# Exchanging 32x32 blocks through device memory in place of transposes on the tensor engine

## The chip, the cores and the metric

The kernel runs on one core of a Trainium2 chip. The metric is the device time of one execution in microseconds (us). A core has a tensor engine (PE, with PEld for its weight loads), a vector engine (DVE), a scalar engine (ACT), GpSimd (POOL) and a sync engine (SP), each with an instruction stream of its own that it works off in order, and 16 DMA engines that move data between device memory and the on-chip buffers.

## The reference

256 tokens of width 2048 go through one transformer block and then two further layers. All weights are float32 and each is used once. In outline:

```
x = x + merged(heads(norm(x) @ w_in)) @ w_out      # 16 MLA heads and 16 forget-gate (fox) heads
x = x + peer(norm(x))                              # product keys over 16384 experts
for layer in 0, 1:
    aq ak av ag bq bk bv bg cu cglu cg = split(x @ w_in2)
    ya = diff_attention(aq, ak, av) * silu(ag)     # 4 heads of 128
    yb = dilated_attention(bq, bk, bv) * silu(bg)  # 8 heads of 128
    yc = conv_module(cu, cglu) * silu(cg)
    x = layer_norm(alpha * x + concat(ya, yb, yc) @ w_out2)
```

In the first block the outputs of the two attentions are multiplied by a sigmoid of a gate before `w_out`; in the layers the outputs of the three branches by a silu. The attention needs queries and keys with the head's dimension on the partitions, and each product with a weight needs its left operand with the contracted dimension on the partitions. Projections come out with the tokens on the partitions, so a block of 256 tokens x 512 columns has to be transposed before it serves as either.

## The kernel before

The weights stream through in 561 jobs, each a tile `raw` of 128 x 2048 floats (1 MB), loaded by SP four tiles ahead. A tile is worked in 4 pieces of 512 columns, 2244 pieces in all. For each piece ACT casts the weights to a short float (`hi`, L208), DVE takes the rest (`lo` = raw - hi, L209), and PE makes three products for each of the two blocks of 128 tokens: hi with the activations' upper part (L260), lo with it (L261), hi with their lower part (L263). Eight buffers for hi and for lo let ACT and DVE run up to 7 pieces ahead of PE.

Everything else (attention, norms, transposes, gates) is side work, written as Python generators. A planner, `Tasks`, takes one step (a tick) after each piece and writes out the next part of at most one task of each of its 4 lanes, so the order on every engine is fixed in advance: `yield n` lets n ticks pass, `apart` is the number of ticks after a task before those that need it may start, and a job that needs a result `flush`es what is left of its task at once. A tick is thus a place in the program, one piece of weights wide.

The change touches these pieces of side work. `transposed` (L223 to L231) transposes four 128x128 blocks at a time on PE into a PSUM tile `side` (L230, 8 instructions for 256 tokens x 512 columns), and hands each of two such tiles on. `to_heads` (L504 to L512) copies these tiles out on ACT, as queries or keys of four heads; `fox_norm`, the MLA tasks `post_q` and `post_k` and the layers' `heads_post` (L1109) call it. `merged_task` (L700) copies gated outputs out as an upper and a lower part, on ACT (L212) and DVE (L213). `split_scaled` and `split` are such pairs of instructions, with and without a factor. `exchange` works in the manner of code that already stands in the part on the experts: two 32x32-block transposes on DVE (L946), a write to device memory (`ad`, L948) and four reads (L957) that bring the blocks back in their transposed places. The softmax of a head (`softmax_block`, L531 to L535) runs on DVE and ACT, with an exponential on ACT between two DVE rows; L1149, L1188, L1152 to L1156 and L1194 belong to the layers' heads, L1224 and L1227 are the taps of the convolution, and L1253 to L1258 the activation after its norm, with ACT and DVE in turn.

Of the kernel before, what the change touches and what calls it, by code (L numbers as in the profile page):

```python
# [110 lines left out]
def hybrid_block_kernel(ctx: ExitStack, tc: tile.TileContext, a: dict, out: bass.AP):  # L111
# [46 lines left out]
    cst = kept([256], name="cst")  # L158
    A.dma_start(out=cst, in_=a["cst"][:, 0:256])
# [11 lines left out]
    ident, maskf = cst[:, 0:128], cst[:, 128:256]  # L171
# [4 lines left out]
    for c0 in (0, 256):  # L176
        V.tensor_copy(out=causal[:, c0:c0 + 128], in_=maskf)
# [291 lines left out]
    def forget_bias(g):  # L469
# [4 lines left out]
        mask = maskf[:, None, :].to_broadcast([P, 4, P])  # L474
# [29 lines left out]
    def to_heads(raw, gain):  # L504

        dst = s4([4, T])
        for pv, c in transposed(lambda c, tb: raw[:, tb, c * P:(c + 1) * P], 4):
            if gain is None:
                A.copy(out=dst[:, c:c + 2, :], in_=pv)
            else:  # L510
                A.activation(out=dst[:, c:c + 2, :], in_=pv, func=AF.Copy, scale=gain)
        return dst  # L512

    def fox_norm(key, raw, gain, post):
        def work():
# [5 lines left out]
            S[key] = to_heads(raw, gain)  # L521
# [34 lines left out]
    def attention(parts, b0, b1, v, y, h):  # L556
# [10 lines left out]
        for tb in range(TB):  # L567
            V.tensor_scalar(out=y[:, tb, h * P:(h + 1) * P], in0=o[:, tb * P:(tb + 1) * P], scalar1=rs[:, tb:tb + 1],
                            scalar2=None, op0=OP.mult)
# [59 lines left out]
    def mla_group(g):  # L629
# [13 lines left out]
        def post_q(ps):  # L643
# [3 lines left out]
            def work():  # L647
# [11 lines left out]
                S["mq", g] = (to_heads(raw, vcol("mq")), rope_T(qr, False))  # L659
# [3 lines left out]
        def post_k(ps):  # L663
# [3 lines left out]
            def work():  # L667
# [11 lines left out]
                S["mk", g] = (to_heads(raw, vcol("mk")), rope_T(kr, True))  # L679
# [20 lines left out]
    def merged_task(key, m, scale):  # L700

        h, l = s4([4, T], F32R), s4([4, T], F32R)
        S[key] = (h, l)

        def work():
            for pv, c in transposed(lambda c, tb: m[:, tb, c * P:(c + 1) * P], 4):
                split_scaled(h[:, c:c + 2, :], l[:, c:c + 2, :], pv, scale)
            yield END
        S[key + ("t",)] = tasks.add(work(), apart=7, lane=1)

    def gate_jobs(kind, g):
# [9 lines left out]
        def post(ps):  # L721
# [7 lines left out]
            merged_task(("m" + kind, g), z, 0.5)  # L729
# [91 lines left out]
    def peer_q_jobs():  # L821
# [5 lines left out]
        for b in range(4):  # L827
            def post(ps, b=b):
# [3 lines left out]
                def work():  # L832
                    qT = to_heads(raw, None)
# [271 lines left out]
    def layer(ly):  # L1105
# [504 lines left out]
```

## Time and profile before

| | |
|---|---|
| time, median of 3 runs | 3291.41 us (3290.26 to 3292.29) |
| the profiled execution: time, span | 3291.13 us, 3289.3 us |
| PE busy | 3258.4 us, 99% of the span |
| PEld busy | 2706.2 us, 82% |
| DVE busy | 2360.8 us, 72% |
| ACT busy | 1748.4 us, 53% |
| POOL busy | 644.8 us, 20% |
| mean granted clock of PE | 0.997 |

The span runs from the first to the last instruction of the core; the profiled execution took 1.83 us more than its span. Busy shares are means over the whole span: an engine at 72% may be full in one stretch and idle in another. Matmuls overlap, so the time that one costs is read from the distance between starts.

### The profile page before, as it was taken

The page shows a single profiled execution, that of the slowest core. Times are in us where ns is not written, and L with a number is a line of the kernel's source. Part 1 is how long each engine was busy: PE and PEld are TensorE (multiplying, and loading weights), DVE is VectorE, ACT ScalarE, POOL GpSimd, SP SyncE. Part 2 cuts the span into 40 slices and gives each one's busy share as a digit, 9 for nine tenths or more (in the row PEclk, how much of TensorE's full clock was granted, in tenths as well). Part 3 has the DMA queues.
Part 4 walks back from the last instruction along what each step waited for, and adds up shares of the span by engine and source line. Part 5 has one row for each costly group of instructions (what it writes and reads, how often), then busy time and mean ns, then how long its engine had stood idle before and what let it go on. Part 6 is the DMA issues. An engine that isn't in the chain of part 4 may idle for free.

```text
span 3289.3 us, 42994 instructions
## 1 busy us (share of the span) xinstructions
PE 3258.4 (99%) x15019; PEld 2706.2 (82%) x15020; DVE 2360.8 (72%) x4733; ACT 1748.4 (53%) x3061; POOL 644.8 (20%) x590
## 2 busy tenths in 40 slices
PE   9999999999999999999999999999999999999997
PEld 7878888888888888888888888888888888788886
DVE  6677676776678888555676766767668777778767
ACT  6655555554655555555554444444555554455553
POOL 0000000000007787876232222220000000000001
PEclk9999999999999999999999999999999999999999
DMA  6544555678557788777788777776564456444454
GB/s 246 174 151 160 182 186 173 210 263 281 174 181 213 216 225 222 212 217 218 258 261 250 238 253 243 231 241 209 203 219 167 154 181 207 171 167 165 172 192 141
DMA packets 159897, 676.54 MB, mean 206 GB/s; under 512 B 52000, under 2 KB 68784, under 8 KB 88128
## 3 DMA queue, kind: packets, MB, share of 16 engines
q1 hardware_dynamic: 102416, 613.06, 55.0%
q0 software_dynamic: 56832, 60.45, 8.7%
q8 instruction: 117, 1.92, 0.2%
q14 instruction: 100, 0.82, 0.1%
q10 hardware_dynamic: 432, 0.29, 0.0%
HBM read 635.58 MB, written 38.15 MB: 205 GB/s over the span
## 4 chain that ended last, share of the span: by engine, by line
PE 98%; DVE 1%; ACT 0%; issue 0%; DMA 0%; DVEq 0%; SPq 0%; ACTq 0%
PE acc L263 31%; PE acc L260 31%; PE acc L261 31%; PE side L230 2%; PE side L576 2%; PE side L542 1%; PE side L552 0%; PE side L553 0%; PE side L551 0%; DVE lo L209 0%; PE side L839 0%; DVE X L1328 0%; DMA X<-in_x_dram 0%; DVE lst L1314 0%; DVE X L295 0%
## 5 line engine op out<-in xcount | busy, mean ns | idle before, releaser
L209 DVE TENSOR_TENSOR lo<-raw,hi 128x512 fp32r<-128x512 f32 x2244 | 1502.5, 688 | 713.0 <-ACT hi L208 699.1
L208 ACT CAST hi<-raw 128x512 fp32r<-128x512 f32 x2244 | 1369.5, 622 | 1166.5 <-DVE lo L209 596.3
L260 PE MATMUL acc<-hi,xh 128*128 128x512 f32 x2816 | 1119.2, 397 | 2.0 <-ACT xh L1362 0.9
L261 PE MATMUL acc<-lo,xh 128*128 128x512 f32 x2816 | 1097.3, 390 | 4.9 <-DVE lo L209 4.9
L263 PE MATMUL acc<-hi,xl 128*128 128x512 f32 x2816 | 1097.9, 390 | 2.9 <-DVE xl L209 2.8
L260 PE MATMUL acc<-hi,s 128*128 128x512 f32 x1664 | 654.3, 393 | 0.0
L261 PE MATMUL acc<-lo,s 128*128 128x512 f32 x1664 | 647.6, 389 | 0.0
L263 PE MATMUL acc<-hi,s 128*128 128x512 f32 x1664 | 646.0, 389 | 0.0
L263 PEld LDWEIGHTS acc<-hi,xl 128*128 128x128 f32 x2816 | 529.0, 188 | 116.1 <-DVE xl L209 4.1
L261 PEld LDWEIGHTS acc<-lo,xh 128*128 128x128 f32 x2816 | 529.7, 188 | 111.3 <-DVE lo L209 6.3
L260 PEld LDWEIGHTS acc<-hi,xh 128*128 128x128 f32 x2816 | 529.5, 188 | 108.3 <-ACT xh L1362 1.6
L914 POOL DMA_INDIRECT gd<-pick x256 | 430.3, 1681 | 93.7 <-issue 74.6
L263 PEld LDWEIGHTS acc<-hi,s 128*128 128x128 f32 x1664 | 312.4, 188 | 65.3
L261 PEld LDWEIGHTS acc<-lo,s 128*128 128x128 f32 x1664 | 312.6, 188 | 63.4
L260 PEld LDWEIGHTS acc<-hi,s 128*128 128x128 f32 x1664 | 312.5, 188 | 63.1
L1339 POOL TENSOR_TENSOR X<-X,s 128x512 f32<-128x512 f32 x6 | 9.0, 1525 | 875.9 <-ACT X L1338 875.9
L957 POOL DMA_DIRECT2D s<-ad x128 | 77.1, 622 | 407.2 <-PE acc L263 189.2
L535 ACT ACTIVATE s<-s,sm 128x128 f32<-128x128 f32 (+1 forms) x128 | 57.2, 448 | 123.3 <-DVE sm L533 123.3
L1227 DVE SCALAR_TENSOR_TENSOR s<-s,vec,s 128x256 f32<-128x256 f32 x240 | 115.5, 481 | 4.5
L948 POOL DMA_DIRECT2D ad<-s x32 | 28.7, 898 | 365.4 <-DVE s L946 364.4
L960 POOL DMA_DIRECT2D s<-gd x128 | 90.5, 713 | 19.1 <-DMA s<-gd 7.7
L984 DVE TENSOR_TENSOR X<-X,acc 128x512 f32<-128x512 f32 x128 | 81.9, 681 | 0.0
(257 smaller groups left out, 1675.1 us busy)
## 6 DMA issues: line engine op xcount, KB each, us to landing
raw<-in_ut_dram SPq DMA_DIRECT2D x128, 1024.0 KB
raw<-in_pv_dram SPq DMA_DIRECT2D x128, 1024.0 KB
raw<-in_w_dram SPq DMA_DIRECT2D x120, 1024.0 KB
raw<-in_win_dram SPq DMA_DIRECT2D x87, 1024.0 KB
raw<-in_wout_dram SPq DMA_DIRECT2D x32, 1024.0 KB
raw<-in_wo_dram SPq DMA_DIRECT2D x32, 1024.0 KB
gd<-s SPq DMA_DIRECT2D x16, 1024.0 KB
raw<-in_wpq_dram SPq DMA_DIRECT2D x16, 1024.0 KB
```

Source lines behind the costliest of these rows:

```text
L208: A.copy(out=hi, in_=src)
L209: V.tensor_tensor(out=lo, in0=src, in1=hi.bitcast(F32), op=OP.subtract)
L230: PE.transpose(pv[:, i, tb * P:(tb + 1) * P], src_of(c + i, tb), ident)
L260: PE.matmul(ps[tb], lhsT=lh[:, kc, t], rhs=wh, start=start, stop=False)
L261: PE.matmul(ps[tb], lhsT=lh[:, kc, t], rhs=wl, start=False, stop=False)
L263: PE.matmul(ps[tb], lhsT=ll[:, kc, t], rhs=wh, start=False, stop=stop)
L576: PE.matmul(sc[:, o0:o0 + k1], lhsT=q[:, q0:q0 + P], rhs=k[:, 0:k1], start=i == 0, stop=i == len(parts) - 1)
L914: G.indirect_dma_start(out=gd.rearrange("p i (n o) -> (p i n) o", o=1), out_offset=bass.IndirectOffsetOnAxis(ap=pick[:, 1, h, k:k + 1].bit ...
L957: G.dma_start(out=aT[32 * q:32 * q + 32], in_=S["ad", g][:, :, q].rearrange("(i r) t x -> r t i x", i=4))
L960: G.dma_start(out=gg[:, q], in_=gd[:, :, g * 4 * 32:(g + 1) * 4 * 32])
L984: V.tensor_tensor(out=X[:, tb, c], in0=X[:, tb, c], in1=ps[tb], op=OP.add)
L1227: V.scalar_tensor_tensor(out=cv[:, c], in0=pad[:, k:k + T], scalar=tapw(k), in1=cv[:, c], op0=OP.mult, op1=OP.add)
```

## The change

A new function `exchange` stands for the PE transposes in `to_heads` and `merged_task`. It transposes the source in blocks of 32x32 on DVE, two instructions of 128x512; writes the result to device memory from POOL's queue (512 KB); reads it back in four transfers of 128 KB into 32 partitions each, into the same buffer; and lets 12 ticks pass. ACT, and for gated outputs DVE, then copy from that buffer in SBUF instead of from PSUM, in one instruction of 128x1024 where there were two of 128x512. 44 blocks go this way: 8 of fox queries and keys, 8 of MLA queries and keys, 12 of the layers' heads, 8 gate merges and 8 merges in the layers. The gated outputs are therefore copied without a factor (but for `oa`), and the factor 0.5 goes into instructions that scale anyway. `merged_task` keeps its successors 2 ticks away instead of 7. At the start a 64 KB load brings the identity alone, and the masks come by two more DMAs instead of two DVE copies. The transposes of the activations, the latents, the rotated parts, the convolution and the experts' queries stay on PE.

```diff
+    def exchange(src):
+        gt = s4([TB, 4, 4, 32])
+        mem = dram.tile([P, TB, 4, P], F32, name=nm("xm"))
+        for tb in range(TB):
+            V.transpose(out=gt[:, tb].rearrange("p q b c -> p b q c"), in_=src[:, tb])
+        G.dma_start(out=mem, in_=gt.rearrange("p t q b c -> p t q (b c)"))
+        back = gt.rearrange("p t i b c -> p t i (b c)")
+        for q in range(4):
+            G.dma_start(out=back[32 * q:32 * q + 32], in_=mem[:, :, q].rearrange("(i r) t x -> r t i x", i=4))
+        yield 12
+        return back.rearrange("p t i (b c) -> p (t i) b c", b=4)
...
-    def to_heads(raw, gain):
-        dst = s4([4, T])
-        for pv, c in transposed(lambda c, tb: raw[:, tb, c * P:(c + 1) * P], 4):
-            if gain is None:
-                A.copy(out=dst[:, c:c + 2, :], in_=pv)
-            else:
-                A.activation(out=dst[:, c:c + 2, :], in_=pv, func=AF.Copy, scale=gain)
-        return dst
+    def to_heads(raw, *gains):
+        back = yield from exchange(raw)
+        dsts = [s4([4, T]) for _ in gains]
+        for dst, gain in zip(dsts, gains):
+            copy_scaled(by_32(dst), back, gain)
+        return dsts if len(dsts) > 1 else dsts[0]
...
-    def merged_task(key, m, scale):
-        h, l = s4([4, T], F32R), s4([4, T], F32R)
-        S[key] = (h, l)
+    def merged_task(key, m, scale=None):
         def work():
-            for pv, c in transposed(lambda c, tb: m[:, tb, c * P:(c + 1) * P], 4):
-                split_scaled(h[:, c:c + 2, :], l[:, c:c + 2, :], pv, scale)
+            back = yield from exchange(m)
+            h, l = s4([4, T], F32R), s4([4, T], F32R)
+            S[key] = (h, l)
+            if scale is None:
+                split(by_32(h), by_32(l), back)
+            else:
+                for b in range(4):
+                    split_scaled(by_32(h)[:, :, b], by_32(l)[:, :, b], back[:, :, b], scale)
             yield END
-        S[key + ("t",)] = tasks.add(work(), apart=7, lane=1)
+        S[key + ("t",)] = tasks.add(work(), apart=2, lane=1)
...
-        def heads_post(name, gain):
+        def heads_post(name, *gains):
...
-                    if name != "ak":
-                        L[name] = to_heads(raw, gain)
-                    else:
-                        L[name] = [s4([4, T]), s4([4, T])]
-                        for pv, c in transposed(lambda c, tb: raw[:, tb, c * P:(c + 1) * P], 4):
-                            for i in range(2):
-                                copy_scaled(L[name][i][:, c:c + 2, :], pv, halves[:, i:i + 1])
+                    L[name] = yield from to_heads(raw, *gains)
                     yield END
                 L[name + "_t"] = tasks.add(work(), apart=11)
```

Since the planner waits in ticks, other side work moves against the weights' pieces. Lines of the changed kernel lie 18 or 19 further down in the layers (L531 is L549, L1152 is L1171, L1227 is L1246) and one up near the start (L209 is L208).

On POOL, in the first block after the write of the forget-gate sums (`fd`), the old order goes on to loads of these sums and of gate biases:

```order
L466 DMA fd<-s_223_999 16x256
L472 DMA s_287_1271<-fd 128x1024
L472 DMA s_587_2441<-fd 128x1024
L719 DMA s_692_2828<-in_bgate_dram 128x512
L719 DMA s_758_3109<-in_bgate_dram 128x512
L472 DMA s_939_3857<-fd 128x1024
```

and in the changed order, at the same place (`xm` is an exchange's tile in device memory, `s` the buffer in SBUF):

```order
L465 DMA fd<-s_223_999 16x256
L513 DMA xm_1156<-s_259_1155 128x1024
L516 DMA s_259_1155<-xm_1156 32x8x128 x4
L471 DMA s_286_1267<-fd 128x1024
L513 DMA xm_1364<-s_308_1363 128x1024
L516 DMA s_308_1363<-xm_1364 32x8x128 x4
```

Exchanges now stand between them; the four reads of an exchange follow its write directly, so on POOL they wait for it.

On DVE, in layer 0, the first place is where the differential heads' two softmaxes are put together (L1152 to L1156; `raw`, `lo` and `hi` are the weights, the other names buffers). Before:

```order
L209 TENSOR_TENSOR lo_23357<-raw_23107,hi_23356 128x512
L209 TENSOR_TENSOR lo_23367<-raw_23107,hi_23366 128x512
L1152 TENSOR_SCALAR sm_23320<-sm_23320,lam_21940 128x2
L1154 TENSOR_SCALAR s_5409_23321<-s_5409_23321,sm_23320 128x128
L1156 SCALAR_TENSOR_TENSOR s_5392_23269<-s_5392_23269,sm_23268,s_5409_23321 128x128
L1154 TENSOR_SCALAR s_5409_23321<-s_5409_23321,sm_23320 128x256
L1156 SCALAR_TENSOR_TENSOR s_5392_23269<-s_5392_23269,sm_23268,s_5409_23321 128x256
L1227 SCALAR_TENSOR_TENSOR s_5182_22342<-s_5154_22236,vec_90,s_5182_22342 128x256 x2
L209 TENSOR_TENSOR lo_23387<-raw_23107,hi_23386 128x512
```

and in the changed order:

```order
L208 TENSOR_TENSOR lo_23436<-raw_23193,hi_23435 128x512
L512 STREAM_TRANSPOSE s_5452_23445<-s_5395_23239 128x4x4x32 x2
L208 TENSOR_TENSOR lo_23455<-raw_23193,hi_23454 128x512
L1171 TENSOR_SCALAR sm_23399<-sm_23399,lam_21884 128x2
L1173 TENSOR_SCALAR s_5439_23400<-s_5439_23400,sm_23399 128x128
L1175 SCALAR_TENSOR_TENSOR s_5422_23348<-s_5422_23348,sm_23347,s_5439_23400 128x128
L1173 TENSOR_SCALAR s_5439_23400<-s_5439_23400,sm_23399 128x256
L1175 SCALAR_TENSOR_TENSOR s_5422_23348<-s_5422_23348,sm_23347,s_5439_23400 128x256
L1246 SCALAR_TENSOR_TENSOR s_5182_22286<-s_5155_22181,vec_90,s_5182_22286 128x256 x2
L208 TENSOR_TENSOR lo_23472<-raw_23193,hi_23471 128x512
```

The two transposes of a key or query block (L512) stand between two weight pieces ahead of L1171. One convolution row, L1224, which came 7 rows further on before, no longer follows.

The second place on DVE is in layer 0 between the statistics of the convolution's norm and its use, before:

```order
L209 TENSOR_TENSOR lo_24624<-raw_24375,hi_24623 128x512
L1194 TENSOR_SCALAR s_5638_24322<-side_24633,sm_24387 128x128 x2
L209 TENSOR_TENSOR lo_24640<-raw_24375,hi_24639 128x512
L1194 TENSOR_SCALAR s_5638_24322<-side_24649,sm_24411 128x128 x2
L209 TENSOR_TENSOR lo_24656<-raw_24375,hi_24655 128x512
L1194 TENSOR_SCALAR s_5638_24322<-side_24665,sm_24437 128x128 x2
L209 TENSOR_TENSOR lo_24672<-raw_24375,hi_24671 128x512
L1194 TENSOR_SCALAR s_5638_24322<-side_24683,sm_24461 128x128 x2
```

and in the changed order, from the transposes of the gated output `oa` on:

```order
L512 STREAM_TRANSPOSE s_5689_24468<-s_5677_24434 128x4x4x32 x2
L1258 BN_STATS sm_24478<-side_24479 128x6
L1259 BN_AGGR sm_24478<-sm_24478 128x2
L1258 BN_STATS sm_24478<-side_24487 128x6
L1259 BN_AGGR sm_24478<-sm_24478 128x2
L208 TENSOR_TENSOR lo_24496<-raw_24304,hi_24495 128x512
L549 ISA s_5700_24510,sm_24511<-side_24505,s_5174_22252 128x128
L549 ISA sm_24511 128x1
L549 ISA s_5700_24510,sm_24511<-side_24505,s_5174_22252 128x256
L549 ISA sm_24511 128x1
L551 TENSOR_SCALAR sm_24512<-sm_24511 128x2
L1207 RECIPROCAL sm_24509<-sm_24508 128x2
```

In place of the last scalings of heads that were done (L1194) stand the softmaxes of the last four heads (L549 to L1207), one between each pair of weight pieces; two rows L213 that followed before are gone, and three copies L562 (L544 before) come in ahead of L1272 (L1253 before). The number of weight pieces in the stretch is the same, and five of them in a row now come ahead of it where there were two between the last copy L544 and it.

## Rows read from the trace of the kernel before

**Rows 1.** The page: busy us and share by engine; the chain that ended last.

```profile
PE 3258.4 (99%) x15019; PEld 2706.2 (82%) x15020; DVE 2360.8 (72%) x4733; ACT 1748.4 (53%) x3061; POOL 644.8 (20%) x590
...
PE 98%; DVE 1%; ACT 0%; issue 0%; DMA 0%; DVEq 0%; SPq 0%; ACTq 0%
```

**Rows 2.** Waits of PE over the span: line, releaser, us in total, times, longest.

```profile
PE acc L261 <- DVE lo L209: 4.9, 4, 2.9
```

**Rows 3.** PE by line and form: instructions, busy us, mean ns; then the chain.

```profile
L230 PE MATMUL side<-cst,s 128*128 128x128 f32 x464 | 59.5, 272 | 0.0
...
478.28 1.31 PE side L230 x12
```

**Rows 4.** Timeline of PE around one group of transposes: start us, us, line.

```profile
340.65 1.04 PE L230 MATMUL side<-cst,s 128*128 128x128 f32 x8
341.44 0.48 PE L260 MATMUL acc<-hi,xh 128*128 128x512 f32 x1
341.76 0.39 PE L261 MATMUL acc<-lo,xh 128*128 128x512 f32 x1
341.99 0.39 PE L263 MATMUL acc<-hi,xl 128*128 128x512 f32 x1
```

**Rows 5.** DVE by line and form: count, busy us, mean ns, idle before it.

```profile
L209 DVE TENSOR_TENSOR lo<-raw,hi 128x512 fp32r<-128x512 f32 x2240 | 1500.8, 688 | 713.0 <-ACT hi L208 699.1 <-issue 7.6 <-ACT s L940 1.9
...
L946 DVE STREAM_TRANSPOSE s<-s 128x512 f32<-128x512 f32 x64 | 45.2, 707 | 6.9 <-ACT s L940 2.6 <-issue 2.0 <-DMA gd<-pick 1.3
...
L544 DVE COPY s<-side 128x384 f32<-128x384 f32 x56 | 30.9, 553 | 1.0 <-PE side L542 1.0
```

**Rows 6.** One group of ACT, in the same columns.

```profile
L208 ACT CAST s<-s 128x1024 fp32r<-128x1024 f32 x32 | 33.6, 1050 | 60.6 <-DVE s L969 56.8 <-DMA s<-ad 1.9 <-DMA s<-gd 1.9
```

**Rows 7.** Timeline rows of POOL: a write and reads of device memory.

```profile
2393.96 0.71 POOL L1064 DMA_DIRECT2D skew<-s  x1 [5.40 <-ACT s L1063]
...
2398.60 0.75 POOL L1070 DMA_DIRECT2D s<-skew  x1 [2.43 <-DMA skew<-s]
...
1685.16 2.42 POOL L957 DMA_DIRECT2D s<-ad  x4 [10.35 <-PE acc L263]
...
1693.27 0.59 POOL L957 DMA_DIRECT2D s<-ad  x1 [1.46 <-DMA s<-ad]
```

**Rows 8.** Timeline of DVE, then PE, after layer 0's differential softmaxes.

```profile
2513.78 0.28 DVE L531 CUSTOM_DVE_ANT_0 s<-side,s 128x128 f32<-128x128 f32 x1
...
2515.67 0.17 DVE L1149 RECIPROCAL sm<-sm 128x2 f32<-128x2 f32 x1 [1.06 <-ACT s L535]
2516.18 1.29 DVE L209 TENSOR_TENSOR lo<-raw,hi 128x512 fp32r<-128x512 f32 x2 [0.35 <-ACT hi L208]
...
2522.79 0.41 DVE L1224 TENSOR_SCALAR s<-s,vec 128x256 f32<-128x256 f32 x1
...
2524.15 1.89 DVE L209 TENSOR_TENSOR lo<-raw,hi 128x512 fp32r<-128x512 f32 x3
...
2525.26 0.39 PE L261 MATMUL acc<-lo,xh 128*128 128x512 f32 x1
```

**Rows 9.** The same, where four softmaxes of heads b0 end.

```profile
2561.10 1.29 DVE L209 TENSOR_TENSOR lo<-raw,hi 128x512 fp32r<-128x512 f32 x2
...
2563.39 0.39 PE L261 MATMUL acc<-lo,xh 128*128 128x512 f32 x1
```

**Rows 10.** Timeline of DVE, then PE, at layer 0's convolution norm.

```profile
2645.24 0.60 DVE L1194 TENSOR_SCALAR s<-side,sm 128x128 f32<-128x128 f32 x2
...
2653.00 1.41 DVE L213 SCALAR_TENSOR_TENSOR s<-side,hg,s 128x512 fp32r<-128x512 f32 x2
...
2656.12 0.99 DVE L1253 TENSOR_SCALAR s<-side,vec 128x256 f32<-128x256 f32 x2
...
2663.51 4.30 DVE L209 TENSOR_TENSOR lo<-raw,hi 128x512 fp32r<-128x512 f32 x7
...
2664.64 0.39 PE L261 MATMUL acc<-lo,s 128*128 128x512 f32 x1
```

More of the change, by code (lines that the diff above doesn't have):

```diff
@@ L157, in hybrid_block_kernel @@
     X = res.tile([P, TB, D], F32, name="X")
-    cst = kept([256], name="cst")
-    A.dma_start(out=cst, in_=a["cst"][:, 0:256])
+    ident = kept([128], name="ident")
+    A.dma_start(out=ident, in_=a["cst"][:, 0:128])
     warm = s2([512], BF16)
@@ L176, in hybrid_block_kernel @@
     for c0 in (0, 256):
-        V.tensor_copy(out=causal[:, c0:c0 + 128], in_=maskf)
+        A.dma_start(out=causal[:, c0:c0 + 128], in_=a["cst"][:, 128:256])
     halves = kept([2], name="halves")
@@ L473, in forget_bias @@
         yield 8
-        mask = maskf[:, None, :].to_broadcast([P, 4, P])
+        mask = causal[:, None, 0:P].to_broadcast([P, 4, P])
         V.tensor_tensor(out=f0, in0=f[:, :, 0:P], in1=mask, op=OP.add)
@@ L520, in work @@
             yield
-            S[key] = to_heads(raw, gain)
+            S[key] = yield from to_heads(raw, gain)
             yield END
@@ L568, in attention @@
             V.tensor_scalar(out=y[:, tb, h * P:(h + 1) * P], in0=o[:, tb * P:(tb + 1) * P], scalar1=rs[:, tb:tb + 1],
-                            scalar2=None, op0=OP.mult)
+                            scalar2=0.5, op0=OP.mult, op1=OP.mult)
         yield END
@@ L658, in work @@
                 yield 9
-                S["mq", g] = (to_heads(raw, vcol("mq")), rope_T(qr, False))
+                qr = rope_T(qr, False)
+                S["mq", g] = ((yield from to_heads(raw, vcol("mq"))), qr)
                 yield END
@@ L678, in work @@
                 yield 9
-                S["mk", g] = (to_heads(raw, vcol("mk")), rope_T(kr, True))
+                kr = rope_T(kr, True)
+                S["mk", g] = ((yield from to_heads(raw, vcol("mk"))), kr)
                 yield END
@@ L728, in post @@
             V.scalar_tensor_tensor(out=z, in0=z, scalar=1.0, in1=y, op0=OP.add, op1=OP.mult)
-            merged_task(("m" + kind, g), z, 0.5)
+            merged_task(("m" + kind, g), z)
         block_jobs([a["win"][b, k] for k in range(4)], post, pre=pre)
@@ L832, in work @@
                 def work():
-                    qT = to_heads(raw, None)
+                    qT = s4([4, T])
+                    for pv, c in transposed(lambda c, tb: raw[:, tb, c * P:(c + 1) * P], 4):
+                        A.copy(out=qT[:, c:c + 2, :], in_=pv)
                     yield
@@ L1264, in pw_post @@
         def pw_post(ps):
-            L["yc"] = raw_of(ps)
+            L["yc"] = raw_of(ps, lambda tb: 0.5)
             L["c_t"] = []
@@ L1299, in layer @@
         outs(0, "oa", first=ALPHA)
-        blk(11, lambda ps: silu_gate(ps, lambda: L["yb", 1], "ob1", 0.5, "b1"))
+        blk(11, lambda ps: silu_gate(ps, lambda: L["yb", 1], "ob1", None, "b1"))
         outs(1, "ob0")
```

15 lines of the change are left out of this document (8 added, 7 removed).

## The prediction

> **What bounds the kernel now.** I read the page's busy shares and the chain first: PE is busy for 99% of the span and carries 98% of the chain [rows 1]. Work taken off PE therefore shortens the time, as long as PE isn't made to wait instead. So the second view is PE's waits: its only mentionable wait on DVE's lower parts is 4.9 us in 4 pieces [rows 2]. The third is DVE, which the change loads. Of its idle time in front of L209, 713.0 us, 699.1 end with ACT's cast [rows 5]: over most of the span DVE has done everything that there is, the eight buffers are full, and it runs at PE's pace. There an added microsecond on DVE costs nothing. But a mean over the span doesn't tell this of a single stretch, so the fourth view sets a weight piece's end on DVE beside its use on PE, at the places where side work is densest. After the differential heads' softmaxes in layer 0, DVE's first of three L209 ends 0.69 us after 2524.15, at 2524.84, and PE uses it at 2525.26 [rows 8]: 0.42 us to spare. At the convolution's norm DVE does no weight piece from 2656.12 to 2663.51; the next one ends at 2664.20, and PE uses it at 2664.64 [rows 10]: 0.44 us. Layer 1 runs the same program, so there are four such places, nearly waits already.
>
> **PE.** A lone group of 8 transposes starts at 340.65, the next product at 341.44, and that product takes 0.32 us to the next start instead of 0.227 (as from 341.76 to 341.99; 6 of them, 1.36 us, make a piece): 0.79 + 0.09 = 0.88 us [rows 4]. An MLA group has 12, of which 4 (the rotated part) stay; it costs 1.31 in the chain [rows 3], and the 4 left about a third, 0.44: 0.87. The change takes away 44 groups of 8, 352 of the instructions whose larger form counts 464 [rows 3]: 44 x 0.875 = **-38.5 us**. Nothing hides this work, since it stands on the engine of the chain. By instruction time, 352 x 272 ns would be 95.7 us [rows 3]; but these durations overlap, and I take the distance between starts.
>
> **DVE, in total.** Added are 88 block transposes at the price of the nearest row, L946, same operation and shape, 707 ns: +62 us; of the L213, L209 and mask rows some are swapped for others of like length. Spread evenly this would go into the 699 us of waiting for ACT [rows 5], and the median stretch takes it for nothing. The price is paid only where DVE is nearly late.
>
> The Trainium skill (VectorE: DVE Perf Modes, Rules for kernel authors, with The three transpose paths) says to put a 128x128 transpose on TensorE if the destination may be PSUM, and that DVE's own transpose turns 32x32 blocks only. Here the destination was PSUM, so the page speaks against the change; by its rule the 62 us on DVE would be the dearer side. Whether that holds is a question of which engine the chain runs on, and is a rival below.
>
> **DVE at the narrow places**, per layer:
> - *After the differential softmaxes.* In the changed order two block transposes stand there, 2 x 0.707 = 1.41 us, and a PE group that gave DVE 0.88 us of time is gone. L1224, 0.41 us [rows 8], has moved away, and 0.42 were to spare: 1.41 + 0.88 - 0.41 - 0.42 = **1.5 us** of wait. Bounds: 0 if all of it falls ahead of a piece with lead; 2.3 with neither credit.
> - *24 pieces on*, where the dilated heads b0 have four softmaxes in a row. The same kind of place, with more to spare: the first of two L209 from 2561.10 ends at 2561.8, and PE uses it at 2563.39, 1.6 us later [rows 9]. 1.41 + 0.88 - 1.6 = **0.7 us**, bounds 0 and 2.3.
> - *The convolution's norm.* Four softmaxes of heads b1 now stand in the stretch. One takes DVE from 2513.78 to 2515.84, 2.06 us, of which 1.06 is a wait for ACT's exponential [rows 8]: 4 x 2.06 = 8.2. Two block transposes 1.4, three copies L562 at 0.47 (553 ns [rows 5], less what overlaps) 1.4. Out go four pairs L1194 at 0.60 [rows 10], 2.4, and two L213 of together 1.3 (1.41 less overlap [rows 10]). Net +7.3 us. Of this 0.4 us were to spare. The softmaxes stood ahead of the stretch before, where five weight pieces now come in a row: DVE can enter with up to two pieces more in its buffers, 2.7 us of PE. 7.3 - 0.4 - 2.7 = **4.2 us**. Bounds: 0 if the waits for ACT (4 x 1.06) are spent on weight pieces that are late anyway; 6.9 if DVE can't get further ahead.
>
> Together 6.4 us a layer, **+12.8 us** for two, bounds 0 and 23. In the first block one fox softmax moves into an already dense stretch and one rotation out; I take 0, within 2 us.
>
> **ACT** copies or casts one 128x1024, 1050 ns in the nearest row [rows 6], where it had two of half the size. At 53% busy [rows 1], and off the chain, that is 0. The start's smaller load and two more DMAs: 0, within 1 us.
>
> **POOL, the queue and the 12 ticks.** POOL was busy 20% [rows 1], and its rows outside the experts' part are few. One exchange, in series: transposes 1.4; the write, from the start of its issue to the read that it releases, 4.6 (2393.96 to 2398.60, the nearest row); four reads issued in 2.4, and the last landed at most 6.9 later (from the end of a read in the middle of the four at 1685.16, about 1686.4, to 1693.27, a wait that ended with such a read, with other traffic about) [rows 7]. That is at most 15.3 us. Twelve ticks are 12 x 1.36 = 16.3 us and whatever side work lies between; and when ACT's copy, which stands 12 pieces later, has to wait, it holds up ACT's casts, but PE feels it only after the pieces that are already cast, 4 or more (5.4 us). So the round trip is covered: 0. Without that cover each exchange would cost its excess over 21.8 us. Reads of one exchange can hold the next one's write on POOL, but exchanges are at least 4 pieces apart for most, and the transfers that follow, the gate biases, are needed much later.
>
> **The sum:** 3291.1 (the profiled execution) - 38.5 + 12.8 = 3265.4, **3265 us**. The profiled execution is 0.3 us below the median of the runs, which changes nothing. A tell-apart limit of 0.2% is 6.6 us: faster is below 3284.8, slower above 3298.0.
>
> **The rivals.**
> - *All of the gain is kept*, 3252.6 us: the added DVE work finds room at the four narrow places too. For it: 699 us of DVE idle behind ACT. Against: 0.42 and 0.44 us to spare there. 0.18.
> - *DVE becomes the bound in more places*, the page's rule: the order that the planner makes puts the added transposes on other dense stretches, in the first block above all. If all 62 us came on PE's path the time would be 3291.1 - 38.5 + 62 = 3314.6; for half of it, 3283.6. For it: DVE, at 72% busy [rows 1], is the next fullest engine. Against: DVE waits for ACT, not PE for DVE, in all but 4 pieces [rows 2]. 0.12, most of it below 3285.
> - *The exchange comes too late* and ends slower: one mechanism, the round trip through the queue. Above 21.8 us each further microsecond costs up to 44. From 22.8 us on (44 us) the gain is gone; at 24, 3291.1 - 38.5 + 97 = 3349. For it: four reads and a write in one software queue beside the weight loads, a landing that no row shows with this size. Against: the rows above add up to 15.3 at most. 0.04.
> - That the groups leave PE and give nothing is excluded by the chain, in which each stands with its 0.88 us.
>
> **Chances.** Forecast (gain less waits of 3 to 23 us): 0.64; its own range is 3255 to 3276. All kept 0.18, DVE bound 0.12, too late 0.04, something unseen 0.02. The range 3250 to 3281 takes in the forecast, the kept gain and the lower part of DVE as a bound, and leaves out about 0.15. Faster: 0.64 + 0.18 + 0.08 + 0.01 = 0.91; same 0.04; slower 0.05.
>
> **What would show it.** L230 down by 352 instructions and some 38 us of starts. PE's wait on DVE's lower parts (now L260) up from 4.9 to some 18 us, in single waits of 1 to 5 us at the three places of each layer, the longest at the convolution's norm; elsewhere none. Block transposes up by 88 at about 0.71 us. ACT's copies behind an exchange without a wait on a DMA. Wrong would be: waits of ACT on DMA by the tens of microseconds, many waits of PE in the first block, or a smaller distance between starts per group than 0.88.

## The result and the profile after

The changed kernel takes 3331.52 us (median of 4 runs, 3320.74 to 3336.68), against 3291.05 us before in the same runs: ratio 1.0118, 95% interval 1.0106 to 1.0131. It is 40 us slower, where 26 us less was forecast. The profiled execution took 3336.68 us.

The page after (span 3334.9 us): the busy engines, and the chain that ended last.

```profile
PE 3249.6 (97%) x14668; PEld 2677.7 (80%) x14668; DVE 2400.4 (72%) x4809; ACT 1735.5 (52%) x3021; POOL 774.5 (23%) x810
...
PE 82%; issue 6%; DVE 5%; DMA 5%; ACT 2%; POOL 1%; SPq 0%; ACTq 0%; DVEq 0%; POOLq 0%
```

PE was 99% busy and carried 98% of the chain [rows 1]; now it carries 82%, and "issue", DVE, DMA and ACT have the rest. The work did leave PE: 352 of the 464 transposes from buffers [rows 3] are gone (line, form, count, busy us, mean ns, idle before).

```profile
L229 PE MATMUL side<-ident,s 128*128 128x128 f32 x112 | 18.3, 299 | 10.9 <-DVE s L1264 9.3 <-DVE s L562 1.5
```

The waits of PE (line, releaser, us in total, times, longest) answer to [rows 2], where the wait for weights' lower parts was 4.9 us, the largest of all.

```profile
PE side L594 <- ACT s L184: 14.2, 3, 6.3
PE acc L259 <- ACT s L207: 11.0, 2, 8.9
PE acc L260 <- DVE lo L208: 10.2, 12, 2.1
PE side L229 <- DVE s L1264: 9.3, 2, 4.7
PE side L560 <- ACT s L553: 6.3, 17, 0.7
PE side L569 <- DVE s L562: 4.4, 4, 1.7
...
PE acc L259 <- ACT hi L207: 1.7, 3, 0.9
```

The wait on weight pieces, L260, has grown from 4.9 to 10.2 us, less than forecast. The larger ones are of another kind: PE stands in front of heads' products (L594) and of products with merged gates (L259) until ACT has copied what an exchange brought back, and in front of transposes (L229) until DVE has normed the convolution. ACT itself waits here:

```profile
ACT s L184 <- DMA s<-xm: 61.6, 16, 9.9
ACT s L207 <- DMA s<-xm: 61.4, 11, 12.6
```

123 us of standing at reads that had not landed, where the prediction had none. While ACT stands it casts no weights, and DVE gets no pieces. But PE hardly ran out of cast pieces: it waited for a cast 3 times, 1.7 us in all (the last of its rows above). What it waited for was the late copy itself, 25.2 us in the first two of its rows, all of it in the first block, before 855 us.

One such place in full: two exchanges close together near 200 us. First DVE's transposes (start, us, line), then POOL's queue.

```profile
197.12 1.30 DVE L512 STREAM_TRANSPOSE s<-s 128x512 f32<-128x512 f32 x2
...
200.71 1.30 DVE L512 STREAM_TRANSPOSE s<-s 128x512 f32<-128x512 f32 x2
```

```profile
198.71 0.58 POOL L513 DMA_DIRECT2D xm<-s  x1 [63.88 <-DVE s L512]
202.60 2.41 POOL L516 DMA_DIRECT2D s<-xm  x4 [3.31 <-DMA xm<-s]
204.91 0.64 POOL L513 DMA_DIRECT2D xm<-s  x1
215.53 2.41 POOL L516 DMA_DIRECT2D s<-xm  x4 [9.98 <-ACT hi L207]
```

The first pair of transposes ends at 198.4, the second at 202.0. POOL writes the first block at 198.71 and stands until it has landed, 3.31 us, before it issues the reads. The second block, ready at 202.0, is written at 204.91, after those reads, and has landed only by 215.53: its reads are issued 13.5 us after its transposes. (The releaser named there, a cast, is not what POOL waits for; the reads need the write.) What ACT and PE do meanwhile:

```profile
207.71 0.62 ACT L207 CAST hi<-raw 128x512 fp32r<-128x512 f32 x1 [0.74 <-PE acc L262]
213.33 1.15 ACT L184 ACTIVATE s<-s,vec 128x1024 f32<-128x1024 f32 x1 [5.00 <-DMA s<-xm]
214.39 2.16 ACT L207 CAST hi<-raw 128x512 fp32r<-128x512 f32 x4
224.96 1.15 ACT L184 ACTIVATE s<-s,vec 128x1024 f32<-128x1024 f32 x1 [8.41 <-DMA s<-xm]
```

```profile
226.16 2.92 PE L594 MATMUL side<-s,s 128*128 128x128 f32 x8 [6.25 <-ACT s L184]
```

ACT's cast ends at 208.3, and the next thing in its order is the first copy: 5.00 us of waiting for the read. Four casts later comes the second copy: 8.41 us. The heads' product L594 needs that copy and starts at 226.16, after 6.25 us with PE idle. Some three pieces of weights were cast and ready meanwhile. This is an estimate: the cast at 207.71 had waited for a buffer, so PE was 8 pieces behind it; until 219.9 PE does 9 more at 1.36 us, and ACT casts 4. PE works in order and could not take them ahead of L594.

### The profile page after: what moved, and what is told of

It is laid out like the page before. It is cut to its first block, busy times and chain, and to the rows that moved or that the text cites. A ratio compares the mean times of both kernels' runs of the same rounds, so it can differ in the third digit from the quotient of the medians.

```text
span 3334.9 us, 42772 instructions
## 1 busy us (share of the span) xinstructions
PE 3249.6 (97%) x14668; PEld 2677.7 (80%) x14668; DVE 2400.4 (72%) x4809; ACT 1735.5 (52%) x3021; POOL 774.5 (23%) x810
## 4 chain that ended last, share of the span: by engine, by line
PE 82%; issue 6%; DVE 5%; DMA 5%; ACT 2%; POOL 1%; SPq 0%; ACTq 0%; DVEq 0%; POOLq 0%
PE acc L262 26%; PE acc L260 26%; PE acc L259 26%; DMA s<-xm 3%; DVE lo L208 2%; DMA xm<-s 1%; ACT hi L207 1%; PE side L594 1%; POOL s L516 1%; PE side L229 1%; DMA raw<-in_win_dram 1%; ACT s L553 0%; DVE s L512 0%; DVE s L549 0%; PE side L569 0%
## 5 line engine op out<-in xcount | busy, mean ns | idle before, releaser
L208 DVE TENSOR_TENSOR lo<-raw,hi 128x512 fp32r<-128x512 f32 x2244 | 1491.2, 686 | 672.8 <-ACT hi L207 656.2
L259 PE MATMUL acc<-hi,xh 128*128 128x512 f32 x2816 | 1121.1, 398 | 3.4 <-ACT hi L207 1.7
L260 PE MATMUL acc<-lo,xh 128*128 128x512 f32 x2816 | 1101.6, 391 | 9.7 <-DVE lo L208 9.3
L259 PE MATMUL acc<-hi,s 128*128 128x512 f32 x1664 | 655.8, 394 | 11.0 <-ACT s L207 11.0
L260 PE MATMUL acc<-lo,s 128*128 128x512 f32 x1664 | 648.5, 390 | 0.8 <-DVE lo L208 0.8
L260 PEld LDWEIGHTS acc<-lo,xh 128*128 128x128 f32 x2816 | 531.6, 189 | 122.5 <-DVE lo L208 16.2
L259 PEld LDWEIGHTS acc<-hi,xh 128*128 128x128 f32 x2816 | 531.6, 189 | 113.7 <-ACT hi L207 3.7
L259 PEld LDWEIGHTS acc<-hi,s 128*128 128x128 f32 x1664 | 313.1, 188 | 75.5 <-ACT s L207 11.8
L260 PEld LDWEIGHTS acc<-lo,s 128*128 128x128 f32 x1664 | 313.2, 188 | 64.4 <-DVE lo L208 1.2
L513 POOL DMA_DIRECT2D xm<-s x44 | 25.6, 582 | 1156.7 <-DVE s L512 1141.0
L516 POOL DMA_DIRECT2D s<-xm x176 | 106.3, 632 | 226.9 <-DMA xm<-s 65.7
L208 DVE TENSOR_TENSOR s<-s,s 128x1024 fp32r<-128x1024 f32 x46 | 56.4, 1225 | 99.2 <-ACT s L207 99.2
L1246 DVE SCALAR_TENSOR_TENSOR s<-s,vec,s 128x256 f32<-128x256 f32 x240 | 115.4, 481 | 4.5
L207 ACT CAST s<-s 128x1024 fp32r<-128x1024 f32 x46 | 48.3, 1050 | 122.3 <-DMA s<-xm 61.4
```

The source lines that it names most:

```text
L207: A.copy(out=hi, in_=src)
L208: V.tensor_tensor(out=lo, in0=src, in1=hi.bitcast(F32), op=OP.subtract)
L259: PE.matmul(ps[tb], lhsT=lh[:, kc, t], rhs=wh, start=start, stop=False)
L260: PE.matmul(ps[tb], lhsT=lh[:, kc, t], rhs=wl, start=False, stop=False)
L516: G.dma_start(out=back[32 * q:32 * q + 32], in_=mem[:, :, q].rearrange("(i r) t x -> r t i x", i=4))
L1246: V.scalar_tensor_tensor(out=cv[:, c], in0=pad[:, k:k + T], scalar=tapw(k), in1=cv[:, c], op0=OP.mult, op1=OP.add)
```

## The experiments

Theory 1: the reads land too late for copies that stand at a fixed place in ACT's order, ACT stops casting, and PE runs dry. It has parts: (1a) exchanges close together wait for each other on POOL's queue, (1b) the transfers are slow, (1c) 12 ticks are far less time on ACT than on PE. Theory 2: DVE is the bound, by the added transposes (2b) or by the softmaxes that moved into the stretch at the convolution's norm (2a). Theory 3: the exchanges' traffic slows the loads of weights. The kernels of the table were timed in four groups (the first four rows, the next four, the next two, the last two), each on one chip, and the changed kernel apart from them; the kernel before was timed with each and took 3291.0 to 3292.5 us.

| kernel | us, median | lowest to highest | ratio to before, 95% |
|---|---|---|---|
| reads elsewhere, no wait | 3283.09 | 3281.56 to 3286.25 | 0.9976 (0.9965, 0.9987) |
| no write, no reads | 3283.11 | 3280.99 to 3285.86 | 0.9974 (0.9963, 0.9986) |
| no block transposes | 3284.25 | 3282.56 to 3289.79 | 0.9981 (0.9971, 0.9990) |
| 20 ticks | 3327.95 | 3325.59 to 3330.29 | 1.0111 (1.0094, 1.0128) |
| heads 3 ticks behind the copies | 3318.41 | 3316.11 to 3326.41 | 1.0087 (1.0070, 1.0104) |
| MLA on PE | 3313.02 | 3311.12 to 3320.42 | 1.0071 (1.0054, 1.0088) |
| reads from ACT's queue | 3345.74 | 3342.78 to 3353.70 | 1.0173 (1.0156, 1.0190) |
| fox and layers alone, 12 ticks | 3297.01 | 3290.36 to 3300.30 | 1.0013 (1.0003, 1.0023) |
| the same, 16 and 24 ticks | 3280.08 | 3279.36 to 3280.51 | 0.9965 (0.9951, 0.9978) |
| no write, no reads, heads 3 ticks behind | 3265.70 | 3265.16 to 3266.82 | 0.9922 (0.9907, 0.9938) |
| layers alone, 16 and 24 ticks | 3278.29 | 3276.78 to 3279.22 | 0.9958 (0.9945, 0.9972) |
| fox, MLA and layers, 16 and 24 ticks | 3278.61 | 3276.71 to 3279.94 | 0.9959 (0.9945, 0.9972) |

**Reads that nobody waits for.** The reads go into another tile of device memory.

```diff
+        far = dram.tile([P, TB, 4, P], F32, name=nm("xn"))
         for q in range(4):
-            G.dma_start(out=back[32 * q:32 * q + 32], in_=mem[:, :, q].rearrange("(i r) t x -> r t i x", i=4))
+            G.dma_start(out=far[32 * q:32 * q + 32], in_=mem[:, :, q].rearrange("(i r) t x -> r t i x", i=4))
```

> The four reads of each exchange go to another tile of device memory instead of back into the buffer, so ACT's copies no longer wait for them; the write, the reads' number and bytes, POOL's queue, DVE's transposes and the order stay (the copies take data that is not exchanged). Theory 1 (reads that land late stop ACT, and with it the casts): the six stalls of PE behind late copies (25.7 us idle) and the half-clock stretches after them (27.2 us, some 10 lost) vanish, about 3296 us, and the stalls at the convolution's norm (4.7 us each) stay. Theory 2 (DVE's added and moved work): no change, 3331 +- 4. Theory 3 (the exchanges' traffic slows the weight loads): no change either.

Measured 3283.09: 48 us less than the changed kernel. No wait of ACT on an exchange is left, nor one of PE on the copy behind an exchange; the largest of PE's waits that are left are at the convolution's norm and on weight pieces:

```profile
PE side L229 <- DVE s L1265: 9.4, 2, 4.7
PE acc L260 <- DVE lo L208: 4.8, 5, 1.8
```

Theory 1 holds in kind, with PE standing at the copy rather than running dry, and is larger than I had put it (36). The two profiled executions are 53.8 us apart. PE's listed waits fall from 67.3 to 30.9 us in all, 25.2 of it the waits at a late copy and the rest short waits elsewhere; the mean granted clock rises from 0.990 to 0.995, worth some 17 us by the reckoning at the end (an estimate). When the 600th piece is cast, behind the attention of the first block, the changed kernel is already 41.8 of the 53.8 us behind. Theories 2 and 3 can't explain these 48 us.

**No transfers at all.** The write and the reads are left out.

```diff
-        G.dma_start(out=mem, in_=gt.rearrange("p t q b c -> p t q (b c)"))
...
-        for q in range(4):
-            G.dma_start(out=back[32 * q:32 * q + 32], in_=mem[:, :, q].rearrange("(i r) t x -> r t i x", i=4))
```

> The exchange's write and reads are left out altogether; transposes on DVE, the 12 ticks and the copies stay (data not exchanged). Theory 1: like the first run, about 3296 us, since only the wait mattered. Theory 2: 3331. Theory 3: the traffic itself mattered, 3296 here but 3331 in the first run. A difference of this run to the first is the price of the traffic and of POOL's queue.

Measured 3283.11, the same as with all the traffic. Theory 3 falls: the 512 KB each way and POOL's issues cost nothing that can be measured here; only being waited for costs.

**No block transposes on DVE.**

```diff
-        for tb in range(TB):
-            V.transpose(out=gt[:, tb].rearrange("p q b c -> p b q c"), in_=src[:, tb])
-        G.dma_start(out=mem, in_=gt.rearrange("p t q b c -> p t q (b c)"))
+        G.dma_start(out=mem, in_=src.rearrange("p t (q c) -> p t q c", q=4))
```

> DVE's 88 block transposes are left out, the write takes the untransposed source, all transfers and waits stay (the copies take data in a wrong arrangement). Theory 1: each round trip is only 1.3 us shorter and the six late places lose at most that each, 3321 to 3331 us. Theory 2: the waits at the dense places of the layers go (10.9 us of idle at the convolution's norm, about 8 on weight pieces, and the half clock after them), about 3305 us.

Measured 3284.25, and neither expectation had it. The edit doesn't do one thing alone: without the transposes a write waits for its source and no longer for its turn in DVE's order, so it leaves earlier by much more than 1.3 us: by 1 to 22 pieces, counted in PE's products (a piece is 1.36 us). Waits of ACT on exchanges fell from 123 to 25 us in this run, which is theory 1's cause taken away by another way. As a price of DVE's added work the run says nothing, and I draw none from it.

**20 ticks instead of 12.**

```diff
-        yield 12
+        yield 20
```

> 20 ticks between the exchange and its copies instead of 12 (10.9 us more for the round trip; the longest wait of ACT on a read was 12.6 us). Side work behind it moves by 8 pieces or is flushed where it is needed. Theory 1: most of the 36 us of the late places come back, about 3297 us, unless a flush puts the copy early again. Theory 2: 3331 +- 8, since DVE has the same work in other places.

Measured 3327.95, hardly less. ACT's waits on exchanges went, as theory 1 says (2.9 and 2.1 us are left); but PE's wait on merged gates grew from 11.0 to 26.7 us, 19.9 of it in one place. POOL, then DVE and ACT there:

```profile
PE acc L259 <- ACT s L207: 26.7, 4, 19.9
```

```profile
708.76 2.41 POOL L516 DMA_DIRECT2D s<-xm  x4 [10.35 <-PE acc L262]
711.07 0.66 POOL L742 DMA_DIRECT2D s<-in_bgate_dram  x1
```

```profile
721.44 1.41 DVE L747 SCALAR_TENSOR_TENSOR s<-acc,rx,s 128x512 f32<-128x512 f32 x2 [12.05 <-DMA s<-in_bgate_dram]
722.88 1.06 ACT L748 ACTIVATE s<-s 128x1024 f32<-128x1024 f32 x1 [14.21 <-DVE s L747]
728.16 1.04 ACT L207 CAST s<-s 128x1024 fp32r<-128x1024 f32 x1 [2.15 <-DMA s<-xm]
```

The products of most gate merges come 15 or 16 pieces after the exchange. With 20 ticks the planner puts the copy right ahead of them, so the wait moved from ACT to PE. Most of the 19.9 us is not the read, though: ahead of the copy in ACT's order stands the next gate's L748, which waits 14.21 us for DVE's L747, and that waits for a gate bias whose load POOL issued only at 711.07, behind another exchange. More ticks help only a result that isn't needed sooner.

**The layers' heads 3 ticks behind the copies.**

```diff
-                L[name + "_t"] = tasks.add(work(), apart=11)
+                L[name + "_t"] = tasks.add(work(), apart=3)
```

> The tasks that need a layer's heads start 3 ticks after the copies instead of 11, so the four softmaxes of the last heads no longer stand between the convolution's norm and its use; all 44 exchanges stay. Theory 2a (the 11 ticks, kept beside the 12 new ones, moved the softmaxes there): the two stalls of 4.7 + 0.8 us and the half clock behind them go, with some waits on weight pieces: 14 to 20 us back, 3312 to 3318 us, all of it in the layers. Rival 2b (the added transposes are too much for DVE wherever the softmaxes stand): PE's waits move elsewhere in the layers, within 5 us of 3331. The stalls of the first block stay in either case.

Measured 3318.41, 13 us less, just short of theory 2a's 14 to 20; the changed kernel's own runs spread over 16 us, but the intervals of the two ratios don't overlap. At the convolution's norm PE's 4.66 and 0.77 us of waiting have become:

```profile
2677.79 1.35 PE L229 MATMUL side<-ident,s 128*128 128x128 f32 x8 [0.62 <-DVE s L1264]
```

That is theory 2a: the last heads' softmaxes are no longer in the stretch, with the same transposes on DVE. Rival 2b falls for this place.

**MLA blocks on PE again.**

```diff
-                S["mq", g] = ((yield from to_heads(raw, vcol("mq"))), qr)
+                S["mq", g] = (by_pe(raw, vcol("mq")), qr)
...
-                S["mk", g] = ((yield from to_heads(raw, vcol("mk"))), kr)
+                S["mk", g] = (by_pe(raw, vcol("mk")), kr)
```

> The 8 MLA blocks are transposed on PE again, 36 exchanges stay; this costs 7 us of PE. Theory 1a (three exchanges close together stand behind each other in POOL's queue, so the second and third are late): the stalls of 6.3, 2.3 and 5.6 us in front of the heads' products and their half clock go, about 20 us back, and with the 7 us 3316 to 3320 us; the stalls at the gate merges (2.1 and 8.9) stay. Theory 1b (any exchange's transfers are late, since the DMA engines are full): little changes but the 7 us, 3331 to 3338.

Measured 3313.02, 18.5 us less in spite of 7 us more on PE. The three stalls in front of heads' products are gone, those at gate merges stay (11.1 us in this run). Theory 1a holds; 1b alone doesn't give this. But the largest stall at a gate merge in the changed kernel, 8.87 us of PE at 854.99, is no case of 1a:

```profile
830.46 1.30 DVE L512 STREAM_TRANSPOSE s<-s 128x512 f32<-128x512 f32 x2
```

```profile
832.06 0.58 POOL L513 DMA_DIRECT2D xm<-s  x1 [15.93 <-DVE s L512]
841.91 2.41 POOL L516 DMA_DIRECT2D s<-xm  x4 [9.27 <-issue]
```

```profile
853.89 1.04 ACT L207 CAST s<-s 128x1024 fp32r<-128x1024 f32 x1 [12.55 <-DMA s<-xm]
```

POOL's last transfer before was at 814.32, and the write is issued 0.3 us after the transposes. It takes 9.85 us until the reads are issued, and the copy follows 12.0 us later: 22.1 us from the transposes' end. The busy share of the DMA engines is given as 0.96 from 832 to 842 us and as 1.02, that is all of it, from 842 to 854. That fits 1b; no run took that load away, so its cause isn't shown.

**Reads from ACT's queue.**

```diff
+        yield 6
         for q in range(4):
-            G.dma_start(out=back[32 * q:32 * q + 32], in_=mem[:, :, q].rearrange("(i r) t x -> r t i x", i=4))
-        yield 12
+            A.dma_start(out=back[32 * q:32 * q + 32], in_=mem[:, :, q].rearrange("(i r) t x -> r t i x", i=4))
+        yield 6
```

> The four reads are issued from ACT's queue 6 ticks after the write, not from POOL's; the copies stay 12 ticks behind the write. No write waits for another exchange's reads any more. Theory 1a (POOL's queue): the stalls of the three close exchanges go without any cost on PE, some 20 us back, about 3311. Theory 1b (the transfers themselves): ACT waits as long for reads issued 6 ticks later, or longer, 3331 or more; and if the write lands later than 6 ticks, ACT stands at the issue instead.

Measured 3345.74, 14 us more. ACT waits less on landed reads, 54 us, but PE more on ACT's exponentials (18.0 us, 6.3 before) and still on the heads' copies (15.3). The queue that orders the transfers now is the one that casts, and issuing holds it up:

```profile
213.98 4.95 ACTq L517 DMA_DIRECT2D s<-xm  x4
```

The next cast starts at 219.03. The 176 issues take 118 us in all, 634 ns each in the median, and ACT is busy for only 21 of them; where the write hasn't landed, ACT stands for it on top. The parts of the 14 us were not separated.

**28 exchanges, 12 ticks.** MLA blocks and gate merges on PE, the layers' heads 3 ticks behind.

```diff
-                S["mq", g] = ((yield from to_heads(raw, vcol("mq"))), qr)
+                S["mq", g] = (by_pe(raw, vcol("mq")), qr)
...
-        S[key + ("t",)] = tasks.add(work(), apart=2, lane=1)
+        if key[0] in ("mm", "mf"):
+            S[key + ("t",)] = tasks.add(on_pe(), apart=7, lane=1)
+        else:
+            S[key + ("t",)] = tasks.add(work(), apart=2, lane=1)
```

> MLA blocks and gate merges on PE again, the 8 blocks of fox queries and keys and the 20 of the layers exchanged, the layers' heads 3 ticks behind the copies. 28 exchanges take 24.5 us off PE. If theories 1 and 2a are the whole loss, neither the late places nor the softmaxes at the convolution's norm are left: 3267 to 3275 us. If 2b holds, some 3280 to 3290.

Measured 3297.01: my theories, as far as they went, were not the whole. No long stall of PE is left in this run, yet ACT stands 78 us behind exchanges (first two rows), and PE has many short waits, more behind ACT's exponentials than of any other kind (third row).

```profile
ACT s L207 <- DMA s<-xm: 41.3, 6, 10.4
ACT s L184 <- DMA s<-xm: 36.5, 13, 6.6
```

```profile
PE side L567 <- ACT s L560: 9.2, 21, 1.6
```

So lone exchanges are late as well. A lone one in the changed kernel, the gated output b0 of layer 0, DVE then ACT, shows why:

```profile
2707.22 1.29 DVE L512 STREAM_TRANSPOSE s<-s 128x512 f32<-128x512 f32 x2
2708.44 4.97 DVE L208 TENSOR_TENSOR lo<-raw,hi 128x512 fp32r<-128x512 f32 x8
```

```profile
2717.50 0.62 ACT L207 CAST hi<-raw 128x512 fp32r<-128x512 f32 x1 [0.74 <-DVE lo L208]
2726.53 1.05 ACT L207 CAST s<-s 128x1024 fp32r<-128x1024 f32 x1 [8.40 <-DMA s<-xm]
```

DVE's transposes end at 2708.5. DVE had been behind, and then does eight pieces in 4.97 us, 0.62 us each, where PE takes 1.36. ACT stands full 7 pieces ahead, so for it the 12 ticks are over at 2718.1: 9.6 us after the transposes, not 16.3. The read lands 18.0 us after them. That is theory 1c for 6.7 of the 8.40 us; the other 1.7 are a round trip longer than 16.3, which is 1b. In the changed kernel the layers' queries and keys that ACT waited for came back 11.6 to 16.3 us after their transposes, so 16.3 us would have covered them; of the nine gated outputs, here and in the first block, that ACT waited for with no other exchange close by, seven took 17.1 to 22.1. Here PE lost little by it, since it didn't need the copy yet and had cast pieces left:

```profile
2729.50 0.50 PE L260 MATMUL acc<-lo,s 128*128 128x512 f32 x1 [0.84 <-DVE lo L208]
```

**The same 28 exchanges with 16 and 24 ticks.**

```diff
-        yield 12
+        yield ticks
...
+        back = yield from exchange(raw, 16)
...
+            back = yield from exchange(m, 24)
```

> The same 28 exchanges as in the run with fox and the layers alone; only the ticks differ: 16 ticks ahead of the copies of queries and keys, 24 ahead of the copies of the layers' gated outputs, whose products come more than 30 pieces later. Theory 1c (12 ticks are not 16.3 us on ACT but some 9 to 13, since DVE, when behind, makes its transposes late and ACT stands full 7 pieces ahead): the waits of ACT for reads, 78 us there, fall below 15 us, and the time by most of what is missing there, to 3267 to 3280 us. Rival (what is missing there is DVE's work): within 5 us of 3297.

Measured 3280.08, 17 us less than with 12 ticks, at the slow end of theory 1c's range. No wait of ACT on an exchange is left, and the rival falls. More ticks cover a slow transfer as well as a short tick, so this run doesn't tell 1c from 1b; the times of the place above do. Of the 24.5 us of PE 11.0 arrive. PE's largest waits now:

```profile
PE side L229 <- DVE s L569: 4.0, 1, 4.0
PE acc L260 <- DVE lo L208: 2.9, 2, 2.7
...
PE side L567 <- ACT s L560: 2.0, 6, 0.7
```

**Both causes away, 44 blocks.** As without transfers, and the heads 3 ticks behind.

> All 44 blocks, without the write and the reads (data not exchanged), and the layers' heads 3 ticks behind the copies: both causes taken away at once. If late reads and the moved softmaxes are separate causes that add up, 3283 less 13 to 20: 3263 to 3270 us, beside 3253 for the whole gain on PE. If one of them only hides the other, it stays above 3278.

Measured 3265.70. Late reads cost 48.4 us with the softmaxes in the stretch at the norm (3331.5 to 3283.1) and 52.7 with the heads 3 ticks behind (3318.4 to 3265.7); the place of the heads costs 13.1 us with the late reads and 17.4 without. The two ways differ by 4 us, less than the changed kernel's spread: two causes that add up. The edit starts all of the heads' tasks sooner, but the listed waits that go are the 10.8 us at the convolution's norm. The rest up to 3252.6, 13.1 us, is taken up below; PE's largest waits in this run, none of these over 1.8 us at a time:

```profile
PE side L565 <- DVE s L558: 5.4, 4, 1.7
PE side L556 <- ACT s L549: 3.9, 12, 0.7
PE acc L260 <- DVE lo L208: 3.6, 4, 1.8
```

**Which exchanges are worth it.** With 16 and 24 ticks: the layers alone, and fox, MLA and layers.

```diff
-            S[key] = yield from to_heads(raw, gain)
+            S[key] = by_pe(raw, gain)
```

> The whole first block on PE, as before the change; the 20 blocks of the layers exchanged, with 16 and 24 ticks. PE gains 17.5 us; the run before this one lost 2 us up to the end of the first block in spite of 8 exchanges there. Theory 1c: no late read and no new stall, 3274 to 3279 us. Rival (fox exchanges are worth their 7 us): 3283 or more.

Measured 3278.29, as expected; of the 17.5 us of PE 14.2 arrive. The 8 fox exchanges win nothing that can be told from the noise: the wait of 4.0 us in the run with them, at 284.93 in the first block, is not in this one.

> As the run with 16 and 24 ticks, and the 8 MLA blocks exchanged too, with 16 ticks. PE gains 7 us more, 3273 us if nothing else changes. Theory 1a (three exchanges within some 10 us on POOL's queue): 16 ticks are too few for the second and third, whose round trips were 22 to 28 us: ACT waits for reads again by some 5 us at a time at these places, and the time comes out above 3280.

Measured 3278.61, 1.4 us under what I had put as the least. The mechanism is the expected one:

```profile
ACT s L184 <- DMA s<-xm: 16.9, 4, 8.9
```

Four late reads, one of 8.9 us. They eat most of the 7 us that PE saves: against the same kernel without the MLA exchanges 1.5 us are left, within the noise. These two are the fastest kernels of the study that do the whole computation, 0.42% and 0.41% below before; the 28 exchanges with 16 and 24 ticks, 0.35% below, can't be told from them.

## Why the prediction was wrong, step by step

- **PE, -38.5 us:** the work did go. With late reads and moved softmaxes both out of the way, 25.3 us of it arrive (3291.0 to 3265.7). Of the other 13 us, some 8 are waits: the listed ones come to 21.2 us in that run and to 13.5 before. They are not of the kind that the prediction counted, since the wait on lower parts is 3.6 us, less than the 4.9 before; the new ones are behind DVE's copies and ACT's exponentials (the first two rows of that run). The last 5 are PE's work: the span less the listed waits falls by 33.6 us at the same mean clock, that is by 0.76 us for each of 44 groups, not 0.875. This is an estimate by subtraction, and what makes a group cheaper was not traced.
- **POOL, the queue and the 12 ticks, 0:** this is the step that failed, worth 48.4 us. The prediction's own sign of being wrong, waits of ACT on DMA by the tens of microseconds, came as 123 us. Three things in it were wrong. *Twelve ticks are 12 x 1.36 us* was wrong: that is their length for PE. For ACT they begin when DVE's transposes end, which is late after a dense stretch, and end when ACT is again as far ahead as the buffers allow; 9.6 us in the place shown. [rows 10] already had DVE's catching up in it, seven pieces in 4.30 us. *Exchanges are at least 4 pieces apart for most* left out MLA's queries and keys, 3.6 us apart in the rows above; the second one then takes 23.0 us, from 202.0 to its copy at 224.96. And *at most 15.3 us*, that is 13.9 after the transposes, was too little for lone ones too, 18.0 and 22.1 in the places shown. In the first of these the write took 4.62 us, as forecast, and the reads 13.1 from their first issue, for 9.3; in the second both took longer than forecast (9.85 and 12.0). *The gate biases are needed much later* held in the changed kernel and failed with 20 ticks.
- **PE feels it only after the pieces that are cast:** right for the weights, which PE waited for by 0.84 us where ACT had stood for 8.40. What it left out is that PE's own next instruction may need the copy: the heads' products and the products of the merged gates did, and PE stood there for 25.2 us with cast pieces ready.
- **DVE at the narrow places, 12.8 us:** the softmaxes that moved cost 17.4 us by the two runs without transfers; I had 8.4 of the 12.8 at the convolution's norm. Place and cause were right, the size was not, and the wait is not on a weight piece: PE's transposes behind the norm stand ahead of all later products, and wait for DVE's L1264. I looked only at the lead of L209 over L261. After the differential softmaxes, with 1.5 us a layer forecast, PE waited 0.66 us a layer where no read was waited for, and 2.1 and 2.3 in the changed kernel; at the place 24 pieces on, with 0.7 forecast, no wait on a lower part is listed.
- **The rivals:** the one that ended slower named the mechanism and got 0.04. It was priced from 21.8 us for each exchange, and so looked far off. DVE as the bound (0.12) explains none of the 48.4 us: with the transposes still on DVE and the reads not waited for, the kernel is faster than before. The rule of the Trainium skill on 128x128 transposes (VectorE: DVE Perf Modes, Rules for kernel authors) points the right way for the change as it was made, but not by DVE's time; the runs show the price in the way back through device memory. Where the copies wait long enough the runs go against the rule: the layers alone with 16 and 24 ticks are 0.42% faster than with the transposes on PE.
- **Transposes on DVE** took 686 ns, for 707 forecast, 88 of them and 57.1 us busy in all.

## What to carry to other kernels

Where a planner places work by ticks, a tick is a place in each engine's order and not a time: the time between two ticks on an engine that runs ahead shrinks when the engine before it is late and catches up, so a transfer has to be covered by the shortest such time, just after the densest stretch. A new latency in a helper has to be answered by those that use it, too: the 11 ticks that had covered the old path stayed beside the 12 new ones and pushed other work into a full stretch. And an in-order queue that writes, waits and reads for one user makes the next one wait for all of it, and any other load that stands behind, as the gate bias did with 20 ticks. A late result costs most where the full engine's next instruction needs it: there a buffer of prepared work doesn't help.

## What the runs showed of the hardware

After the idle time shown here PE does not come back at full speed. At the convolution's norm (start, us, line, and the wait; then windows with busy time by engine and the granted clock, PEclk):

```profile
2684.20 1.36 PE L229 MATMUL side<-ident,s 128*128 128x128 f32 x4 [4.66 <-DVE s L1264]
2686.32 1.11 PE L229 MATMUL side<-ident,s 128*128 128x128 f32 x4 [0.77 <-DVE s L562]
...
2687.66 0.63 PE L260 MATMUL acc<-lo,xh 128*128 128x512 f32 x1
2688.08 0.63 PE L262 MATMUL acc<-hi,xl 128*128 128x512 f32 x1
```

```profile
2678.00:2682.00 4.00, 1.53 (x9) 1.03 (x7) 2.50 (x13) 2.90 (x8) 0.00 (x0) 1.00 0.00 0
2682.00:2686.00 4.00, 1.36 (x4) 0.68 (x4) 3.69 (x13) 0.67 (x2) 0.00 (x0) 0.58 0.75 264
2686.00:2690.00 4.00, 3.68 (x14) 3.09 (x15) 3.30 (x7) 0.59 (x1) 0.00 (x0) 0.56 0.27 61
2690.00:2694.00 4.00, 4.00 (x20) 3.31 (x19) 2.47 (x5) 1.31 (x3) 0.00 (x0) 1.00 0.48 201
```

In the window in which the wait of 4.66 us ends the granted clock is 0.58 of full, in the next one 0.56: for most of both it is the lower level, 1.2 GHz. Products start 0.42 us apart there instead of 0.227. Over the span the mean granted clock is 0.990, against 0.997 before: with the levels 1 and 0.5, some 67 us at the lower one instead of some 20. If PE had worked all through these 47 us more, they would have cost 24 (an estimate); so a part of the loss is not in any list of waits. The Trainium skill (TensorE: Matmul & The Clock Gate, Part 1) has the same two levels and an idle engine that falls to the lower; the trace agrees.

The changed kernel's runs spread over 16 us, where those of before spread over 2; without the reads being waited for the spread was 5. That would fit landing times that vary and show in the result once the chain waits for them; it was not shown run by run.
